# A two-layer diffusion backbone: the seven-product stage with its residual in SBUF and one pair of column blocks per piece

## The chip, the cores and the metric

The kernel runs on one core of a Trainium2 chip. Its engines, as the profile names them, are PE (TensorE; PEld is its loading of weights), DVE (VectorE), ACT (ScalarE), POOL (GpSimd) and SP (SyncE, which here only issues transfers). The metric is the device time of one execution in microseconds (us); of several runs the median counts. A profiled execution is one further run, with its own time; its span goes from the first to the last instruction.

## The reference

Two layers work on 512 latent tokens and 256 context tokens of width 1024. Each layer is a mixing part and a SwiGLU feed-forward part, each behind an RMSNorm whose scale, shift and gate ("modulation") come from `SiLU(cond) @ w_mod`. All is float32. In the last layer the context leaves no output, so only the latent tokens go through its out-projection and feed-forward part. Cut to what matters here:

```python
D_MODEL = 1024; SEQ = 512; CTX_LEN = 256; DEPTH = 2; D_FF = 2816; N_MOD = 6

def swiglu(h, w_gate, w_up, w_down):
    return (jax.nn.silu(h @ w_gate) * (h @ w_up)) @ w_down

def hybrid_layer(x, xc, mod, mod_c, ..., ctx_out):
    sh1, sc1, g1, sh2, sc2, g2 = [mod[:, i] for i in range(N_MOD)]
    ...                                        # three kinds of mixing heads
    x = x + g1 * (jnp.concatenate([y_a, y_b, y_c], axis=-1) @ w_out)
    x = x + g2 * swiglu(modulate(x, norm2_g, sh2, sc2), w_gate, w_up, w_down)
    if ctx_out:                                # the same for xc, in layer 0
        ...
    return x, xc
# for each layer: mod = silu(c) @ w_mod[l] + b_mod[l]; then hybrid_layer; at the end rms_norm(x, final_g)
```

## The kernel before, in words

**Precision.** Every matrix product is made of three: each float32 operand is split into a high part `hi` and a rest `lo`, and TensorE adds hi·hi, hi·lo and lo·hi. For weights, `wload` (L127) does it: SP loads a tile of 128 x 1024 into a slot of the pool `wraw` (four slots), ACT copies it to `whi` (L133), DVE subtracts to get `wlo` (L134); `whi` and `wlo` have three buffers each. `split` (L112 to L114) does the same for tokens and for combined weights.

**Order.** The program is one list of instructions, laid out by hand in Python; each engine runs its part of the list in order, and a tile framework puts in the waits: an instruction that needs a slot of a pool waits until the former user of the slot is done. Transfers queue on the engine that issues them, so a waiting one holds up all behind it.

**Tokens.** The residual x lives in eight tiles, one for each block k of 128 of the 1024 features, with 768 token columns: 256 of the context and 512 latent ones in a tile (`xsl`, L1104, gives a group's columns). `resid` (L1110 to L1114) adds a finished product from PSUM, times the gate row of modulation, onto x, one DVE instruction for each block and token group.

**The seven-product stage** is the feed-forward part of layer 0, `ffn_seven` (L1352). The 2816 columns of w_gate and w_up are 22 blocks of 128, taken in 11 pairs. For a pair, the product of [even, odd feature blocks] by [two column blocks] with the tokens, cut into two halves of 384, is a 2 x 2 block product; it is made with seven block products in place of eight (a Strassen-Winograd scheme). A `Unit` (L1222) does that for the gate (`up` 0) or the up-projection (`up` 1) of one pair: it loads two w_seven tiles, forms sums of weight blocks on DVE (`sums`, L1247; L1250 to L1252), splits them, runs seven products of 12 matmuls 128 x 384 (`prod`, L1265), and puts SiLU(gate) x up into the tiles gh and gl (`put`, L1293). The token operands of the seven products (T1 to T4, B11, B21, B22 for four j) are made once, by `token_sums` and `operands` (L1188, L1196).

After some pairs their part of w_down follows: a *down* (L1360). For each of the eight output blocks k it runs `dense` (L142) over the columns of the piece, two PSUM tiles (512 latent, 256 context columns), alternating between the PSUM pools mm (three tiles) and mx (four), and adds onto x. `FF0_PIECES` (L27) says which pairs go together: one pair, then five times two. The stages of the next unit are woven into the list: its first three products are ahead of the down, the others behind it.

In the stage SBUF is full: the token operands and the gh and gl of two pairs leave no room for x. So x goes to DRAM (`xd`) at the end of the norm (L1178), and in each of the first five downs, for each k, POOL loads `xs` from xd (L1452), DVE adds onto it, and POOL stores it back (L1454). The sixth, last down brings x back (L1461) and runs through `lagged` (L1117): all eight k of the latent tokens, with those of the context trailing behind, so that the next layer's norm of the latent tokens can start while TensorE still works. `TRAIL` says how many trail and after how many of them the norm is begun. Its sums of squares are added on POOL (L264).

**Fill.** The modulation of layer 1 is worked off as filler: `mod_steps` (L210) makes one item for each load of a 128 x 1024 tile of w_mod into a `wraw` slot (L220), one DVE product with accumulated sum (L223), and, for the last of a vector, two small ones. In this stage its items are loaded on POOL's queue. Vectors 0 to 4 of layer 1 (56 items) are issued in the downs: one for each k of the first down, one or two by turns for each k of the next four, 12 in all for each. Vector 5 (8 items) is worked off in layer 1's out-projection, on SP's queue, where `dense` takes one item at each call.

The lines that the diff touches, with the functions that call them:

## Time and profile before

| what | value |
|---|---|
| median of 3 runs | 1766.45 us (1765.04 to 1768.68) |
| profiled execution | 1771.83 us, span 1769.2 us |
| mean granted TensorE clock | 0.965 |
| PE busy | 1641.7 us (93% of the span) |
| DVE busy | 1121.1 us (63%) |
| ACT, POOL busy | 696.3 us (39%), 249.1 us (14%) |
| HBM read, written | 204.31 MB, 26.21 MB |
| the seven-product stage from its first down to the end of its last | 517.58 to 1064.87 us |

How to read the rows that follow: a group names line, engine, operation, `out<-in` by the program's names, shape and count; behind the bar stand its busy time, the mean ns of one, the time that its engine sat idle just ahead of it and what ended that. "Idle" of an engine that is not the bottleneck costs nothing. A row of waits gives the total, how often, and the longest. The granted clock is in shares of full speed, in the page's slices in tenths. Numbers behind a name tell buffers apart.

### The profile page before, as it was taken

Reading aid. Unit: us, or ns where it says so; the run is one execution under the profiler, and the core shown is the slowest. Engines: PE = TensorE matmul, PEld = TensorE weight load, DVE = VectorE, ACT = ScalarE, POOL = GpSimd, SP = SyncE. Lnnn points to the kernel's source line nnn. Section 1 sums busy time; section 2 is a strip of 40 time slices with the busy share of each in tenths; the row PEclk is TensorE's granted clock in tenths of the full one; section 3 lists DMA queues with packets and bytes.
Section 4 is the critical chain, followed back from the end, with each engine's and each line's share of the span. In section 5 each row is a group of like instructions: output and inputs, shape, how many; then the busy total and the mean of one; then the engine's idle time right before and its main releaser. Section 6 shows DMA issues by size and latency. Waiting matters only on the chain.

```text
span 1769.2 us, 26551 instructions
## 1 busy us (share of the span) xinstructions
PE 1641.7 (93%) x10520; PEld 1437.6 (81%) x10520; DVE 1121.1 (63%) x1987; ACT 696.3 (39%) x1277; POOL 249.1 (14%) x309
## 2 busy tenths in 40 slices
PE   7998989899887989899898999989989999999998
PEld 5876777778776969789797988867878988888888
DVE  5598788776875757666575757575597633333335
ACT  5454344643632414133241445534455522222225
POOL 0011022242211020211202030012143100000000
PEclk9998999999897999999898999989999999999999
DMA  8751323234336283653727452211225333222222
GB/s 310 244 152 60 120 79 93 69 117 139 129 120 226 93 272 112 218 186 127 259 79 256 139 185 88 93 57 37 73 91 172 107 99 99 97 99 95 96 78 84
DMA packets 67563, 232.24 MB, mean 131 GB/s; under 512 B 8688, under 2 KB 10352, under 8 KB 67312
## 3 DMA queue, kind: packets, MB, share of 16 engines
q1 hardware_dynamic: 51696, 163.44, 28.2%
q0 software_dynamic: 15744, 67.12, 11.5%
q8 instruction: 82, 1.34, 0.3%
q14 instruction: 41, 0.34, 0.1%
HBM read 204.31 MB, written 26.21 MB: 130 GB/s over the span
## 4 chain that ended last, share of the span: by engine, by line
PE 56%; DVE 15%; issue 14%; DMA 9%; ACT 3%; POOL 2%; DVEq 0%; SPq 0%; POOLq 0%; ACTq 0%
PE dps L157 35%; DMA wmod<-in_w_mod 5%; PE wps L413 4%; PE X L1271 3%; DMA wraw<-in_w_dn 3%; PE vps L659 3%; DVE wlo L134 2%; PE Z L1271 1%; DVE wmod L223 1%; PE ptps L595 1%; PE bops L553 1%; PE Y L1271 1%; DMA wraw<-in_w_seven 1%; PE bsps L553 1%; DVE wlo L114 1%
## 5 line engine op out<-in xcount | busy, mean ns | idle before, releaser
L133 ACT ACTIVATE whi<-wraw 128x1024 fp32r<-128x1024 f32 (+3 forms) x182 | 183.4, 1008 | 511.1 <-PE dps L157 241.0
L134 DVE TENSOR_TENSOR wlo<-wraw,whi 128x1024 fp32r<-128x1024 f32 (+3 forms) x182 | 214.6, 1179 | 155.2 <-ACT whi L133 152.6
L157 PE MATMUL dps<-gh,whi 128*128 128x512 f32 (+1 forms) x576 | 182.0, 359 | 41.0 <-ACT whi L133 41.0
L157 PE MATMUL dps<-gl,whi 128*128 128x512 f32 (+1 forms) x576 | 180.0, 355 | 0.0
L157 PE MATMUL dps<-gh,wlo 128*128 128x512 f32 (+1 forms) x576 | 178.2, 352 | 0.3 <-DVE wlo L134 0.3
L223 DVE SCALAR_TENSOR_TENSOR wmod<-wmod,c_all 128x1024 f32<-128x1024 f32 x96 | 122.6, 1280 | 47.5 <-DMA wmod<-in_w_mod 46.8
L157 PEld LDWEIGHTS dps<-gh,whi 128*128 128x128 f32 x576 | 104.2, 200 | 58.3 <-ACT whi L133 44.2
L157 PE MATMUL dps<-ll,whi 128*128 128x512 f32 x336 | 136.6, 407 | 1.4 <-DVE ll L114 1.4
L157 PE MATMUL dps<-lh,whi 128*128 128x512 f32 x336 | 137.0, 409 | 0.3 <-DVE ck L796 0.3
L157 PE MATMUL dps<-lh,wlo 128*128 128x512 f32 x336 | 135.8, 405 | 0.0
L157 PE MATMUL dps<-h2lh,whi 128*128 128x512 f32 (+1 forms) x336 | 128.0, 384 | 0.0
L157 PE MATMUL dps<-h2ll,whi 128*128 128x512 f32 (+1 forms) x336 | 128.0, 384 | 0.0
L157 PE MATMUL dps<-h2lh,wlo 128*128 128x512 f32 (+1 forms) x336 | 127.9, 384 | 0.0
L157 PEld LDWEIGHTS dps<-gl,whi 128*128 128x128 f32 x576 | 103.8, 199 | 14.8 <-DVE gl L114 0.2
L157 PEld LDWEIGHTS dps<-gh,wlo 128*128 128x128 f32 x576 | 102.8, 197 | 15.3 <-DVE wlo L134 1.2
L1113 DVE SCALAR_TENSOR_TENSOR x<-dps,modT,x 128x256 f32<-128x256 f32 (+1 forms) x80 | 46.9, 589 | 102.5 <-PE dps L157 98.9
L113 ACT ACTIVATE whi<-wraw 128x1024 fp32r<-128x1024 f32 (+1 forms) x66 | 60.0, 914 | 79.9 <-DMA wraw<-in_w_seven 33.3
L157 PE MATMUL dps<-ch,whi 128*128 128x256 f32 x256 | 76.8, 300 | 12.2 <-DVE bv L532 8.0
L1271 PE MATMUL X<-ol,whi 128*128 128x384 f32 x242 | 81.9, 338 | 3.1 <-DVE ol L114 3.1
L1271 PE MATMUL X<-oh,whi 128*128 128x384 f32 x242 | 81.8, 338 | 1.3 <-ACT gate L1290 0.9
L1271 PE MATMUL X<-oh,wlo 128*128 128x384 f32 x242 | 81.5, 337 | 1.0 <-DVE wlo L114 1.0
L157 PE MATMUL dps<-ch,wlo 128*128 128x256 f32 x256 | 75.6, 295 | 3.5 <-DVE wlo L134 3.5
(387 smaller groups left out, 3954.3 us busy)
## 6 DMA issues: line engine op xcount, KB each, us to landing
wmod<-in_w_mod POOLq DMA_DIRECT2D x56, 512.0 KB, 4.6
wraw<-in_w_seven SPq DMA_DIRECT2D x44, 512.0 KB, 4.0
wmod<-in_w_mod SPq DMA_DIRECT2D x40, 512.0 KB, 3.7
wraw<-in_win_blk SPq DMA_DIRECT2D x34, 512.0 KB, 3.6
xs<-xd POOLq DMA_DIRECT2D x40, 384.0 KB, 5.1
xd<-xs POOLq DMA_DIRECT2D x40, 384.0 KB, 5.2
wraw<-in_w_out SPq DMA_DIRECT2D x23, 512.0 KB, 3.3
wraw<-in_w_dn SPq DMA_DIRECT2D x22, 512.0 KB, 4.8
```

The costliest lines, as they stand in the source:

```text
L113: ac.activation(out=hi, in_=src, func=AF.Copy)
L114: ve.tensor_tensor(out=lo, in0=src, in1=hi.bitcast(F32), op=ALU.subtract)
L133: ac.activation(out=hi[:, 0:n], in_=raw[:, 0:n], func=AF.Copy)
L134: ve.tensor_tensor(out=lo[:, 0:n], in0=raw[:, 0:n], in1=hi[:, 0:n].bitcast(F32), op=ALU.subtract)
L157: m = te.matmul(out=ps[:, 0:T], lhsT=wt[:, c], rhs=(flo if wh else fhi)(k), start=(k == 0 and wi == 0), stop=(k == nk - 1 and wi == 2),)
L223: ve.scalar_tensor_tensor(out=wraw.tile([128, D], F32, tag="w", name="junk") if t < ts[-1] else raw, in0=raw, scalar=1.0, in1=c_all[:, t, ...
L413: m = te.matmul(out=ps[:, 0:T], lhsT=wt[:, cs_], rhs=(flo if wh else fhi)(k), start=(k == 0 and wi == 0), stop=(k == KD - 1 and wi == 2))
L553: m = te.matmul(*args, **kw)
L595: te.transpose(out=tps[:, i * 128:(i + 1) * 128], in_=pt[:, i * 128:(i + 1) * 128], identity=ident)
L659: te.matmul(out=vps[i][:, 0:408], lhsT=tokslice(nm, k, i), rhs=wt[:, cs], start=(k == 0 and wi == 0), stop=(k == KD - 1 and wi == 2))
L1113: ve.scalar_tensor_tensor(out=xs, in0=ps, scalar=modT[:, row * 8 + k, g[3]:g[3] + 1], in1=xs, op0=ALU.mult, op1=ALU.add)
L1271: m = te.matmul(out=ps[:, 0:HN], lhsT=wt[:, c], rhs=O[op, j][wh], start=(start and j == 0 and wi == 0), stop=(j == 3 and wi == 2), skip_gr ...
```

## The change

- **Pieces.** `FF0_PIECES` becomes eleven pieces of one pair, so there are eleven downs, ten of the first kind and the last through `lagged`. gh and gl of only one pair are held at a time.
- **Residual.** x stays in its SBUF tiles. The 40 loads and 40 stores of xs, the eight stores of x into xd and the eight loads back go; `resid` adds onto x itself. With eleven downs there are 176 residual adds in the stage where there were 96.
- **w_down's layout.** A 128 x 1024 tile now holds four k of one pair, so a down loads two tiles, each once.
- **Token operands.** For j = 3, T3's hi and lo share one tile, T4 goes into a spare slot (4) of the context's operand tiles, and T1 takes ordinary tiles: 13 tiles of the pool `zc`, none of `za`.
- **Fill.** In the stage only vectors 0 to 2 of layer 1 remain, 40 items, still on POOL's queue: one in each unit and two in each down (at k = 1 and 5). Vectors 3 and 4 (16 items) take the place of vector 5 in layer 1's out-projection, and vector 5 (8 items) goes into the first piece of layer 1's feed-forward part, both on SP's queue.
- **Tail.** `TRAIL[1]`, which the last down uses, goes from (5, 2) to (7, 1).

```diff
-FF0_PIECES = [(0, 2)] + [(f, 4) for f in range(2, 22, 4)]
+FF0_PIECES = [(f, 2) for f in range(0, 22, 2)]
...
-TRAIL = [(7, 1), (5, 2), (4, 2), (4, 2)]
+TRAIL = [(7, 1), (7, 1), (4, 2), (4, 2)]
...
-        def resid(pss, k, row, gs, xt=None):
+        def resid(pss, k, row, gs):
             for ps, g in zip(pss, gs):
-                xs = xsl(k, g) if xt is None else xt[:, goff(g):goff(g) + g[2]]
+                xs = xsl(k, g)
                 ve.scalar_tensor_tensor(
                     out=xs, in0=ps, scalar=modT[:, row * 8 + k, g[3]:g[3] + 1], in1=xs, op0=ALU.mult, op1=ALU.add)
...
-                else:
-                    gp.dma_start(out=xd[k], in_=x[k][:, 0:768])
...
+                if j == 3 and which == "T3":
+                    o3 = zct("o3", F32R)
+                    split(o3[:, n1], o3[:, n2], t[:, n1])
+                    O["T3", j] = (o3[:, n1], o3[:, n2])
+                    split(ch_[:, 4, :], cl_[:, 4, :], t[:, n2])
+                    O["T4", j] = (ch_[:, 4, :], cl_[:, 4, :])
+                    continue
...
                 def dload(k):
-                    if k // 2 not in cache:
-                        cache.clear()
-                        cache[k // 2] = wload(A["w_dn0_%d" % pi][k // 2])
-                    c = (k % 2) * nf * 128
-                    return [t[:, c:c + nf * 128] for t in cache[k // 2]]
+                    if k // 4 not in cache:
+                        cache[k // 4] = wload(A["w_dn0_%d" % pi][k // 4])
+                    c = (k % 4) * nf * 128
+                    return [t[:, c:c + nf * 128] for t in cache[k // 4]]
...
                         u.stage2b()
+                        feed(1)
                         nxt = units[nu + i + 1] if nu + i + 1 < len(units) else None
...
                     for k in range(KD):
-                        xt = zat("xs")
-                        gp.dma_start(out=xt, in_=xd[k])
-                        resid(dense(dload(k), nf, [gpart(g) for g in whole], mm if k % 2 == 0 else mx), k, 5, whole, xt)
-                        gp.dma_start(out=xd[k], in_=xt)
-                        feed(1 + k % 2 if pi else 1)
+                        resid(dense(dload(k), nf, [gpart(g) for g in whole], mm if k % 2 == 0 else mx), k, 5, whole)
+                        if k % 4 == 1:
+                            feed(1)
                     pin[0] = last_pe[0]
                 else:
                     feed(len(fill))
-                    x = x_tiles()
-                    for k in range(KD):
-                        gp.dma_start(out=x[k][:, 0:768], in_=xd[k])
...
-        fill.extend(mod_steps(l, (5,)))
+        fill.extend(mod_steps(l, (3, 4) if last else (5,)))
...
-            fill.extend(mod_steps(1, range(5), True))
+            fill.extend(mod_steps(1, range(3), True))
...
         hp2 = [hpart(h2, g) for g in groups]
-        while fill:
-            fill.pop(0)()
+        feed(len(fill))
+        fill.extend(mod_steps(1, (5,)))
```

How this moves instructions, at the places that matter. First DVE, where the second down begins. Before, ahead of that down's first residual add and behind it (L1300 and L1296 are the last unit's `put`, L134 the w_down split, L223 a modulation item, L1113 a residual add):

```order
L134 TENSOR_TENSOR wlo<-wraw,whi 128x1024
L114 TENSOR_TENSOR gl<-gate,gh 128x384
L1296 TENSOR_TENSOR sn<-sn,Z 128x384
L223 SCALAR_TENSOR_TENSOR wmod,modT<-wmod,c_all 128x1024
L1300 TENSOR_TENSOR gate<-gate,sn 128x384
L114 TENSOR_TENSOR gl<-gate,gh 128x384
L223 SCALAR_TENSOR_TENSOR wmod,modT<-wmod,c_all 128x1024 x2
L1113 SCALAR_TENSOR_TENSOR xs<-dps,modT,xs 128x512
L1113 SCALAR_TENSOR_TENSOR xs<-dps,modT,xs 128x256
L134 TENSOR_TENSOR wlo<-wraw,whi 128x1024
```

And in the change (the lines of `put` are now L1305 and L1301):

```order
L134 TENSOR_TENSOR wlo<-wraw,whi 128x1024
L114 TENSOR_TENSOR gl<-gate,gh 128x384
L1301 TENSOR_TENSOR sn<-sn,Z 128x384
L223 SCALAR_TENSOR_TENSOR wmod,modT<-wmod,c_all 128x1024
L1305 TENSOR_TENSOR gate<-gate,sn 128x384
L114 TENSOR_TENSOR gl<-gate,gh 128x384
L134 TENSOR_TENSOR wlo<-wraw,whi 128x1024
L223 SCALAR_TENSOR_TENSOR wmod,modT<-wmod,c_all 128x1024
L1113 SCALAR_TENSOR_TENSOR x_4159<-dps,modT,x_4159 128x512
L1113 SCALAR_TENSOR_TENSOR x_4159<-dps,modT,x_4159 128x256
L114 TENSOR_TENSOR wlo<-wraw,whi 128x1024
```

The place of the `put` is the same; the second w_down split comes ahead of the first residual add, and one item has left the place ahead of it. Further on in the same down of the change, between the add of block 3 and that of block 7, stand the next unit's split and its sums of weight halves (L1255 to L1257):

```order
L114 TENSOR_TENSOR wlo<-wraw,whi 128x1024
L1113 SCALAR_TENSOR_TENSOR x_4163<-dps,modT,x_4163 128x512
L1113 SCALAR_TENSOR_TENSOR x_4163<-dps,modT,x_4163 128x256
L1255 TENSOR_TENSOR s_5880<-wraw 128x512
L1113 SCALAR_TENSOR_TENSOR x_4164<-dps,modT,x_4164 128x512
L1113 SCALAR_TENSOR_TENSOR x_4164<-dps,modT,x_4164 128x256
L1256 TENSOR_TENSOR s_5881<-s_5880,wraw 128x512
L1257 TENSOR_TENSOR wraw<-wraw 128x512
L1113 SCALAR_TENSOR_TENSOR x_4165<-dps,modT,x_4165 128x512
L1113 SCALAR_TENSOR_TENSOR x_4165<-dps,modT,x_4165 128x256
L223 SCALAR_TENSOR_TENSOR wmod,modT<-wmod,c_all 128x1024
```

They are the next unit's work, which DVE now has within the shorter down. Second POOL's queue. Before, in the first downs, loads and stores of xs stand among the items:

```order
L1452 DMA xs<-xd 128x768 x2
L220 DMA wmod<-in_w_mod 128x1024 x4
L1454 DMA xd<-xs 128x768
L220 DMA wmod<-in_w_mod 128x1024 x2
L1454 DMA xd<-xs 128x768
```

In the change POOL's queue in the stage, from the sums of squares of the norm ahead of it to those of the last down, reads:

```order
L264 TENSOR_TENSOR sqacc<-sqacc,sq 128x256 x6
L220 DMA wmod<-in_w_mod 128x1024 x40
L645 MEMSET v_9617 128x12
L645 MEMSET v_9618 128x12
L645 MEMSET v_9619 128x12
L264 TENSOR_TENSOR sqacc<-sqacc,sq 128x512 x6
```

All transfers of x have gone from it, and nothing else has come in their place.

More of the change, by code (lines that the diff above doesn't have):

```diff
@@ L1203, in operands @@
                 else:
-                    hi, lo = [(zat if j == 3 else zct)(nm, F32R)[:, 0:2 * HN] for nm in ("oh", "ol")]
+                    hi, lo = [zct(nm, F32R)[:, 0:2 * HN] for nm in ("oh", "ol")]
                 split(hi, lo, t[:, 0:2 * HN])
@@ L1352, in ffn_seven @@
         def ffn_seven():
-            nonlocal x
             pairs = [p for f0, nf in FF0_PIECES for p in range(f0 // 2, (f0 + nf) // 2)]
@@ L1617, in layout @@
         "w_seven": np.stack([blocks(w)[0].reshape(22, 128, 8, 128)[:, :, KORD].reshape(22, 128, 1024) for w in (wg, wu)]),
-        **{"w_dn0_%d" % i: blocks(wd[:, f * 128:(f + n) * 128])[0].reshape(4, 2, 128, n * 128).transpose(0, 2, 1, 3).reshape(
-            4, 128, 2 * n * 128) for i, (f, n) in enumerate(FF0_PIECES)},
+        **{"w_dn0_%d" % i: blocks(wd[:, f * 128:(f + n) * 128])[0].reshape(2, 4, 128, n * 128).transpose(0, 2, 1, 3).reshape(
+            2, 128, 4 * n * 128) for i, (f, n) in enumerate(FF0_PIECES)},
         "win_av": ksplit(wi[:, :, 256:512], 4), "w_out": blocks(I["w_out"]), "w_gate": blocks(wg), "w_up": blocks(wu),
```

## The prediction

> **What bounds the kernel now.** I read the page first, for the engine shares, the clock and the transfers.
>
> ```profile
> PE 1641.7 (93%) x10520; PEld 1437.6 (81%) x10520; DVE 1121.1 (63%) x1987; ACT 696.3 (39%) x1277; POOL 249.1 (14%) x309
> PEclk9998999999897999999898999989999999999999
> wmod<-in_w_mod POOLq DMA_DIRECT2D x56, 512.0 KB, 4.6
> xs<-xd POOLq DMA_DIRECT2D x40, 384.0 KB, 5.1
> ```
>
> TensorE is busy for 93%, so what it loses is the rest, and the slices where its clock falls below 9 count too, because there it is busy but slow. Of the six such slices three, the deepest among them, lie between 517 and 977 us, in the seven-product stage. Next comes the view that splits time windows by engine, cut at the starts and ends of the downs (the dense second half of each piece) and of the units between them. Its columns are the length, busy time and count of PE, PEld, DVE, ACT and POOL, the granted clock, the DMA share and GB/s.
>
> ```profile
> 517.58:550.52 32.94, 21.73 (x97) 18.31 (x97) 18.04 (x30) 3.33 (x5) 10.07 (x19) 0.79 0.74 245
> 550.52:615.70 65.18, 62.02 (x340) 61.33 (x339) 45.35 (x73) 28.36 (x48) 3.53 (x7) 0.95 0.37 122
> 615.70:660.26 44.56, 36.38 (x193) 30.93 (x191) 25.69 (x41) 5.55 (x6) 12.00 (x22) 0.92 0.80 270
> 660.26:719.86 59.60, 58.89 (x338) 58.45 (x337) 43.75 (x68) 26.73 (x46) 3.27 (x6) 1.00 0.35 116
> 719.86:765.76 45.90, 38.16 (x194) 32.58 (x194) 25.69 (x41) 5.67 (x6) 12.00 (x22) 0.89 0.80 263
> 765.76:826.20 60.44, 58.92 (x339) 58.44 (x338) 44.10 (x72) 26.96 (x46) 3.27 (x6) 1.00 0.35 114
> 826.20:872.24 46.04, 38.47 (x193) 32.88 (x193) 24.77 (x40) 5.67 (x6) 12.01 (x22) 0.89 0.81 262
> 872.24:931.72 59.48, 58.79 (x338) 58.47 (x337) 44.66 (x70) 26.96 (x46) 3.27 (x6) 1.00 0.36 116
> 931.72:977.00 45.28, 38.67 (x194) 32.93 (x194) 25.97 (x42) 4.65 (x6) 12.00 (x22) 0.89 0.81 267
> 977.00:1029.97 52.97, 51.46 (x297) 50.99 (x296) 36.33 (x59) 25.13 (x41) 4.57 (x11) 1.00 0.46 153
> 1029.97:1064.87 34.90, 34.90 (x203) 30.34 (x202) 20.52 (x30) 16.14 (x27) 14.03 (x11) 1.00 0.49 162
> ```
>
> The units run with TensorE nearly full. The five downs that pass x through DRAM (rows 1, 3, 5, 7 and 9, together 214.7 us, nine pairs) have the clock at 0.79 to 0.92 and the DMA engines at 0.74 to 0.81. The sixth, which keeps x in SBUF, has neither fault. The groups of instructions on TensorE and the waits of every engine in the stage say what is late; the last row is from the waits of SP's DMA queue alone.
>
> ```profile
> L157 PE MATMUL dps<-gh,whi 128*128 128x512 f32 (+1 forms) x342 | 102.0, 369 | 41.0 <-ACT whi L133 41.0
> ACT whi L133 <- DMA wraw<-in_w_dn: 148.5, 15, 14.8
> POOL xs L1452 <- DMA xd<-xs: 73.6, 24, 7.3
> SPq L130 <- DVE wmod L223: 207.9, 15, 19.0
> ```
>
> TensorE waits 41.0 us for split weights, the split waits for the w_dn load, and that load is not issued until a modulation item gives its wraw slot back. The items themselves queue on POOL behind the x transfers. The chain of waits, inside the second down, shows one round of it (start, length, what): item, its product, and only then the load of weights, eleven us from end to end.
>
> ```profile
> 622.80 4.44 DMA wmod<-in_w_mod
> 627.33 1.24 DVE wmod L223 x2
> 628.63 5.45 DMA wraw<-in_w_dn
> ```
>
> **The change, part by part.** *The downs.* I take the unhindered speed from TensorE's timeline; a row "x2" is one 512-column and one 256-column matmul.
>
> ```profile
> 518.64 0.51 PE L157 MATMUL dps<-gh,whi 128*128 128x512 f32 x2
> 519.68 0.51 PE L157 MATMUL dps<-gh,whi 128*128 128x512 f32 x2
> ...
> 545.66 0.84 PE L157 MATMUL dps<-gh,wlo 128*128 128x512 f32 x2
> 548.22 0.73 PE L157 MATMUL dps<-gh,whi 128*128 128x512 f32 x2
> ```
>
> Three pairs of matmuls take 519.68 − 518.64 = 1.04, so 0.347 each. A down of one column pair has 8 k × 2 blocks × 3 products = 48 of them: 16.6 us. After a stall they run at (548.22 − 545.66) / 4 = 0.64. Of the nine pairs' 214.7 us, 9 × 16.6 = 149.8 is work and 64.9 is loss: 41.0 of idle time and 23.9 mostly at the slow rate.
>
> What held the loads goes away by three edits with one answer: the 80 transfers of xs and 16 of x leave POOL's queue, only 4 modulation items are issued per pair (one per unit, two per down) where a two-pair down issued 12 within itself, and a down needs two w_dn loads, queued right behind the w_seven loads. The bytes of w_dn stay about the same. I take the whole loss away: **−64.9**.
>
> *The units.* The three windows of four full units at clock 1.00 give 59.48 to 60.44; the one behind the first down took 65.18, with starved splits at its start. All at the best value: 297.7 (rows 2, 4, 6, 8, 10) to 4 × 59.48 + 52.97 = 290.9, **−6.8**. Per unit the DVE has about what it had (some 44 us per four units) plus one item of 1.31 each (1.223 and the read of its accumulator, 0.08), so 49 of 59.5: covered by TensorE, and 1.3 per unit if that cover failed.
>
> *New friction at ten downs.* What DVE does in a down comes from its groups by shape in the stage:
>
> ```profile
> L1113 DVE SCALAR_TENSOR_TENSOR xs<-dps,modT,xs 128x512 f32<-128x512 f32 x40 | 29.9, 749 | 21.3 <-PE dps L157 16.6 <-DMA xs<-xd 4.4
> L1113 DVE SCALAR_TENSOR_TENSOR xs<-dps,modT,xs 128x256 f32<-128x256 f32 x40 | 19.0, 475 | 0.0
> L134 DVE TENSOR_TENSOR wlo<-wraw,whi 128x1024 fp32r<-128x1024 f32 x22 | 27.2, 1235 | 28.9 <-ACT whi L133 28.9
> L223 DVE SCALAR_TENSOR_TENSOR wmod<-wmod,c_all 128x1024 f32<-128x1024 f32 x56 | 68.3, 1223 | 46.5 <-DMA wmod<-in_w_mod 46.2
> L1252 DVE TENSOR_TENSOR wraw<-wraw 128x512 f32<-128x512 f32 x21 | 14.4, 683 | 0.0
> ```
>
> From its first to its last add a down of one pair now has 8 × (0.749 + 0.475) = 9.8 of adds (per pair twice as many, since each add took in two pairs), two splits for the next unit 2.5, two items 2.6 and three sums of weight halves 2.0: 16.9, for 16.6 of TensorE. Neighbours overlap by some 0.07 (below: 1.23 long, and the next starts 1.16 later), 1.6 over 23 instructions, which leaves about 1.3 of slack. Ahead of the first add stand the last `put`, one split and one item, and PSUM lets TensorE run two k (4.2 us) ahead of the adds. Lower bound of what is lost: 0. Upper bound: one split and one item, 2.5, plus the first add's 0.75, so about 3 per down, if the item's load comes late. The second down of before starts behind much the same order:
>
> ```profile
> 612.68 1.23 DVE L223 SCALAR_TENSOR_TENSOR wmod<-wmod,c_all 128x1024 f32<-128x1024 f32 x1 [0.30 <-DMA wmod<-in_w_mod]
> 613.84 0.56 DVE L1300 TENSOR_TENSOR gate<-gate,sn 128x384 f32<-128x384 f32 x1
> ```
>
> The item held DVE there just ahead of the `put` that the down needs, and its load made DVE wait only 0.30, so I stay nearer the lower bound: 1.0 at each of ten downs, **+10** (0 to 30).
>
> *The tail.* The last down has one pair now and its sums of squares stay on POOL:
>
> ```profile
> L264 POOL TENSOR_TENSOR sqacc<-sqacc,sq 128x512 f32<-128x512 f32 x6 | 8.6, 1440 | 15.6 <-ACT sq L263 15.6
> ```
>
> A k of the 512 latent columns takes 6 × 0.347 × 512 / 768 = 1.39 for one pair, just less than POOL's 1.44: eight adds now end behind TensorE, where two pairs (2.8) left POOL idle between adds. TRAIL (7, 1) leaves seven context denses of 0.7 behind, one of them ahead of the wait. If nothing hides it: 0.4 of accumulated lag, ACT's square, one add and the scale, some 4 twice. I take **+4** (0 to 8).
>
> *Layer 1.* Sixteen modulation items more run there, on SP's queue, 8 more in the out-projection and 8 in the first FFN piece: 16 × 1.31 = 21 us of DVE.
>
> ```profile
> 1360.00:1380.00 20.00, 20.00 (x171) 20.00 (x169) 9.91 (x13) 8.07 (x13) 9.67 (x8) 1.00 0.42 134
> 1480.00:1769.00 289.00, 282.99 (x1398) 238.89 (x1396) 108.62 (x134) 85.07 (x121) 0.00 (x0) 1.00 0.28 92
> ```
>
> DVE has 10 of 20 free there, and over half of the FFN, with TensorE full: nearly all is covered. What is queued behind a waiting item is the next w_out load on SP's queue, and behind its product on DVE the split of that load, so the upper bound is half the 21: **+2** (0 to 10). The 13 packed operand tiles cost one split more, ahead of the first down; I put it at nothing.
>
> *Sum*: −64.9 − 6.8 + 10 + 4 + 2 = −55.7. The profiled execution took 1771.83, 5.4 above the runs' median of 1766.45; 1771.8 − 55.7 = 1716.1, less 5.4 is **1710 us**.
>
> **The rivals.** *A: w_dn is still late.* All three kinds of load still share four slots, so the second w_dn tile can wait for an item. For it: the 207.9 us that SP's queue waited were for items. Against: an item now meets no x transfers. One stall per down, of the shortest of the old ten:
>
> ```profile
> 739.56 0.81 PE L157 MATMUL dps<-gh,whi 128*128 128x512 f32 x2 [2.79 <-ACT whi L133]
> 740.16 0.84 PE L157 MATMUL dps<-gl,whi 128*128 128x512 f32 x2
> ```
>
> Each costs 2.8 and its slow matmuls, 23.9 / 10 = 2.4: 10 × 5.2 − 10 = 42 more, 1752 us. The Trainium skill, "TensorE: Matmul & The Clock Gate", Part 1, puts the fall to half clock behind about 3.4 us of idleness; by that such stalls would cost their idle time alone, which would make A an estimated 1728. The trace disagrees: behind 2.79 us the matmuls run at 0.6 to 0.66.
>
> *B: DVE sets the downs.* If the 16.9 of the means is the truth, nothing is left to catch up in, and the 2.5 of split and item come back as a PSUM wait at each down: 10 × 2.5 − 10 = 15 more, 1725 us. Against: the overlap of neighbours, which the rows show.
>
> *C: the wait moves to layer 1.* 16 items share the slots with w_out and FFN weights there. In the downs, 64.9 us were lost around 56 items, 1.16 each: 16 × 1.16 − 2 = 17 more, 1727 us. Against: the eight that ran there before left TensorE full.
>
> *D, the slower side: short PSUM waits halve the clock in the downs.* With DVE this tight TensorE can pause at every second k, and matmuls at 0.64 instead of 0.347 cost 0.293 each. Slower than before begins where the gain, 55.7 / 10 = 5.6 per down, is eaten: 19 of 48 slow. With half of each down slow, 240 × 0.293 = 70 more, it would take 1780 us. Against: stalls like this one, in the units, left their windows at 0.95 to 1.00.
>
> ```profile
> 556.57 0.69 PE L1271 MATMUL X<-olh,wlo 128*128 128x384 f32 x1 [0.98 <-DVE wlo L114]
> ```
>
> The Trainium skill, same page, "A second HAM failure mode: psum-queue depth-cycling", tells of this in another kernel: pauses between groups, each short, made the clock oscillate. No run here shows it yet.
>
> The downs of before have no stall of this kind, so their rows can't exclude D; it gets little.
>
> **How the numbers follow.** Forecast 0.60, A 0.12 (1752), B 0.14 (1725), C 0.08 (1727), D 0.06 (1780). This kernel's times tell about 0.2% (3.5 us) from no change. A to C and the forecast are faster; one in a hundred goes from A, and one from D, to no change, the rest of D to slower: faster 0.93, same 0.02, slower 0.05. Low end: friction, tail and layer 1 at nothing give 1694, and up to 4 more if the units' start stalls vanish, so 1690. High end: beyond C and the friction's upper bound (1730), and into A, 1745. That leaves out most of A and D.
>
> **What would show it.** Right: no idle time of the downs' matmuls behind L133, ten downs of 16.6 to 18 us with clock 1.00, their DMA share near the units' 0.35, POOL's queue with modulation items alone. A shows as TensorE idle for L133 again; B as DVE at full in the downs and TensorE idle for a residual add; C as TensorE idle for weights between the out-projection and the first FFN piece; D as clock under 0.95 in downs whose stalls are all short. The tail shows as idle time before the sum-of-squares matmul at the end of layer 0. The forecast is wrong if the downs sum to over 200 us, or if the units grow.

## The result

| what | before | after |
|---|---|---|
| median | 1765.74 us (4 runs) | 1708.88 us (4 runs, 1707.05 to 1712.0) |
| ratio, 95% interval | | 0.9677, 0.9658 to 0.9695 |
| profiled execution, span | 1771.83, 1769.2 us | 1707.05, 1705.4 us |
| mean granted TensorE clock | 0.965 | 0.983 |

The change makes the kernel 3.2% faster; the forecast was 1710 us. From the page of the changed kernel, the slices of the clock and the transfers that have changed:

```profile
PEclk9998999999899999999999999989999999999999
wmod<-in_w_mod POOLq DMA_DIRECT2D x40, 512.0 KB, 3.8
wraw<-in_w_dn SPq DMA_DIRECT2D x22, 512.0 KB, 3.3
```

The dips of the clock in the stage are gone, an item of the stage lands in 3.8 us instead of 4.6, a w_dn tile in 3.3 instead of 4.8. TensorE's group of the downs' first product, up to the last down, and the windows by stage (the columns are those of the prediction; first two of the ten downs, then the last unit with the wait behind it and the last down, then two of the nine windows of two units):

```profile
L157 PE MATMUL dps<-gh,whi 128*128 128x512 f32 x160 | 63.7, 398 | 0.7 <-DVE x L1113 0.5
```

```profile
512.88:529.56 16.68, 16.68 (x97) 14.69 (x97) 15.20 (x25) 3.13 (x5) 1.06 (x2) 1.00 0.50 159
652.19:669.75 17.56, 17.52 (x97) 14.78 (x97) 16.38 (x26) 3.38 (x5) 1.06 (x2) 1.00 0.47 150
...
948.59:973.71 25.12, 21.39 (x123) 20.75 (x121) 15.36 (x27) 11.04 (x19) 0.37 (x3) 1.00 0.32 106
973.71:999.67 25.96, 24.84 (x121) 20.92 (x121) 14.13 (x23) 11.82 (x22) 12.08 (x11) 0.87 0.28 101
529.56:558.90 29.34, 29.34 (x170) 29.34 (x169) 21.06 (x34) 12.80 (x22) 1.06 (x2) 1.00 0.29 91
576.02:605.37 29.35, 29.35 (x171) 29.35 (x169) 20.23 (x34) 12.74 (x22) 1.05 (x2) 1.00 0.27 90
```

TensorE no longer waits for split w_dn weights at all (41.0 us before). The ten downs sum to 171.55 us, 17.2 each, at clock 1.00; the units are full. What is left lies behind them: in the row of the last down (973.71 to 999.67) the clock is 0.87.

To set the terms of the sum against the traces a mark is needed that both have behind the stage. It is TensorE's first wait for L686 in layer 1, here from its timelines, before and after:

```profile
1149.15 0.82 PE L693 MATMUL rowps<-cst,f 128*64 128x128 f32 x6 [1.85 <-DVE f L686]
```

```profile
1083.87 0.81 PE L693 MATMUL rowps<-cst,f 128*64 128x128 f32 x6 [1.85 <-DVE f L686]
```

| term | forecast | measured | how |
|---|---|---|---|
| downs, at nine pairs | −64.9 + 10 | −59.8 | 214.7 to 171.55 − 16.64 |
| units | −6.8 | −11.4 | 297.7 to 286.3, without the stall at 973.71 |
| tail | +4 | +10.6 | end of the last unit to the mark: 119.18 to 113.17, and one pair (16.64) less in it |
| layer 1 | +2 | +1.5 | mark to the end: 620.05 to 621.53 |
| ahead of the first down | 0 | −4.7 | 517.58 to 512.88 |

They add up to the 63.8 us between the two spans. The last row is no gain of the change: 4.5 of the 4.7 us were there in the same matmul at 388.8 and 384.3, ahead of every transfer that the change takes away (the first starts at 405.0), and in the variants below the first down began anywhere between 511.8 and 518.2. The forecast's 5.4 us between the profiled execution of before and the median stood for this.

### The profile page after: what moved, and what is told of

The parts are those of the page before. It is cut to its first block, busy times and chain, and to the rows that moved or that the text cites. A ratio compares the mean times of both kernels' runs of the same rounds, so it can differ in the third digit from the quotient of the medians.

```text
span 1705.4 us, 26357 instructions
## 1 busy us (share of the span) xinstructions
PE 1617.9 (95%) x10520; PEld 1418.7 (83%) x10520; DVE 1156.9 (68%) x2064; ACT 693.9 (41%) x1274; POOL 184.8 (11%) x197
## 4 chain that ended last, share of the span: by engine, by line
PE 68%; DVE 15%; issue 8%; DMA 3%; ACT 3%; POOL 2%; DVEq 0%; SPq 0%; POOLq 0%; ACTq 0%
PE dps L157 40%; PE X L1276 8%; PE wps L413 3%; PE Z L1276 3%; PE vps L659 3%; DMA wmod<-in_w_mod 3%; PE Y L1276 2%; DVE wlo L134 2%; PE ptps L595 1%; DVE wmod L223 1%; PE bops L553 1%; PE bsps L553 1%; DVE junk L223 1%; DVE nm L580 1%; ACT whi L133 1%
## 5 line engine op out<-in xcount | busy, mean ns | idle before, releaser
L133 ACT ACTIVATE whi<-wraw 128x1024 fp32r<-128x1024 f32 (+2 forms) x178 | 180.9, 1017 | 357.5 <-PE dps L157 237.0
L134 DVE TENSOR_TENSOR wlo<-wraw,whi 128x1024 fp32r<-128x1024 f32 (+2 forms) x178 | 212.5, 1194 | 122.6 <-ACT whi L133 117.9
L1113 DVE SCALAR_TENSOR_TENSOR x<-dps,modT,x 128x512 f32<-128x512 f32 (+1 forms) x240 | 136.8, 602 | 88.7 <-PE dps L157 87.7
L157 PE MATMUL dps<-gh,whi 128*128 128x512 f32 (+1 forms) x576 | 173.2, 346 | 4.3 <-ACT gh L113 3.0
L157 PE MATMUL dps<-gh,wlo 128*128 128x512 f32 (+1 forms) x576 | 170.6, 341 | 0.0
L157 PE MATMUL dps<-gl,whi 128*128 128x512 f32 (+1 forms) x576 | 170.4, 341 | 0.0
L223 DVE SCALAR_TENSOR_TENSOR wmod<-wmod,c_all 128x1024 f32<-128x1024 f32 x96 | 122.5, 1277 | 20.2 <-DMA wmod<-in_w_mod 19.8
L157 PE MATMUL dps<-lh,wlo 128*128 128x512 f32 x336 | 135.0, 402 | 0.0
L157 PEld LDWEIGHTS dps<-gl,whi 128*128 128x128 f32 x576 | 97.7, 189 | 13.3 <-DVE gl L114 0.5
L157 PEld LDWEIGHTS dps<-ll,whi 128*128 128x128 f32 x336 | 65.0, 193 | 16.2 <-issue 2.2
L114 DVE TENSOR_TENSOR wlo<-wraw,whi 128x1024 fp32r<-128x1024 f32 (+1 forms) x66 | 69.8, 1058 | 11.5 <-ACT whi L113 11.5
L157 PEld LDWEIGHTS dps<-lh,whi 128*128 128x128 f32 x336 | 64.7, 193 | 14.9 <-issue 1.9
```

The costliest lines, as they stand in the source:

```text
L114: ve.tensor_tensor(out=lo, in0=src, in1=hi.bitcast(F32), op=ALU.subtract)
L133: ac.activation(out=hi[:, 0:n], in_=raw[:, 0:n], func=AF.Copy)
L134: ve.tensor_tensor(out=lo[:, 0:n], in0=raw[:, 0:n], in1=hi[:, 0:n].bitcast(F32), op=ALU.subtract)
L157: m = te.matmul(out=ps[:, 0:T], lhsT=wt[:, c], rhs=(flo if wh else fhi)(k), start=(k == 0 and wi == 0), stop=(k == nk - 1 and wi == 2),)
L223: ve.scalar_tensor_tensor(out=wraw.tile([128, D], F32, tag="w", name="junk") if t < ts[-1] else raw, in0=raw, scalar=1.0, in1=c_all[:, t, ...
L1113: ve.scalar_tensor_tensor(out=xs, in0=ps, scalar=modT[:, row * 8 + k, g[3]:g[3] + 1], in1=xs, op0=ALU.mult, op1=ALU.add)
```

## The experiments

**Which edit did it: the fill or the transfers of x?** The prediction gave one answer for three edits. Four kernels take them apart. First the fill alone, on the kernel before:

```diff
                         u.stage2b()
+                        feed(1)
...
-                        feed(1 + k % 2 if pi else 1)
+                        if k % 2 == 1 and (pi or k % 4 == 1):
+                            feed(1)
...
-            fill.extend(mod_steps(1, range(5), True))
+            fill.extend(mod_steps(1, range(3), True))
```

(and vectors 3 to 5 in layer 1 as in the change).

> The kernel before with the change's fill alone: 40 items in the stage, one per unit, two in the first down and four in each two-pair down, and the other 16 and 8 moved into layer 1 as in the change; x still goes through DRAM, pieces of two pairs stay. Theory P (items hold the wraw slots and queue behind the x transfers; it takes both to make w_dn late): TensorE's idle time for split w_dn weights falls from 41.0 to 5 to 15 us, the downs from 214.7 to about 175, the time to 1720 to 1735. Rival S (the number of items in four slots is all of it): idle under 5, time 1712 to 1720. Rival R (the x transfers keep the DMA engines busy and so make the loads slow, whatever the items do): idle stays above 25, time 1745 or more.

Measured: 1712.6 us, ratio 0.9709 (0.9690 to 0.9729). TensorE's group in its stage, and one of its two-pair downs:

```profile
L157 PE MATMUL dps<-gh,whi 128*128 128x512 f32 (+1 forms) x352 | 99.1, 344 | 9.1 <-DVE xs L1113 9.0
```

```profile
602.68:637.42 34.74, 33.97 (x193) 29.35 (x193) 22.43 (x34) 5.24 (x7) 8.66 (x16) 1.00 0.80 257
```

No wait for weights is left, with all 80 transfers in place and the DMA engines as busy as before (0.80); the 9.0 us left are for residual adds. The thinner fill alone brings 52 of the 57 us. That is what S had forecast, in idle time and in time; P had expected 5 to 15 us of idle time and 1720 or more. R falls: busy DMA engines by themselves were not what made the weights late.

Next the opposite, the dense fill of before in the changed kernel:

```diff
-                        if k % 4 == 1:
+                        if k % 4 != 3:
                             feed(1)
...
-            fill.extend(mod_steps(1, range(3), True))
+            fill.extend(mod_steps(1, range(5), True))
```

(without the item per unit, and with layer 1's fill as before).

> The changed kernel with the fill of before: 56 items in the downs, six in each one-pair down, none in the units, and only 8 items in layer 1 (out-projection). x stays in SBUF. Theory P: an item without x transfers ahead of it turns its slot round in about 4.5 + 1.3 us, so w_dn is late by less than before: idle for split weights 10 to 25 us, time 1725 to 1740. Rival S: idle near 41 and the slow clock back, 1750 or more. Rival R: no idle for weights, time 1706 to 1714; DVE's 6 items of 1.3 us in a 16.6 us down then show as PSUM waits only.

Measured: 1711.44 us, ratio 0.9697 (0.9679 to 0.9715):

```profile
L157 PE MATMUL dps<-gh,whi 128*128 128x512 f32 (+1 forms) x352 | 96.3, 347 | 6.0 <-ACT gh L113 3.0 <-DVE x L1113 2.6
```

No wait for weights here either, so S falls too as it was put, and P had the size wrong: dense items beside the change's other edits cost some 2.5 us, not 16 to 31. R had this time in its range, but the run before has ruled out its mechanism. Then the stores of x put back into the changed kernel, and then both together:

```diff
                         resid(dense(dload(k), nf, [gpart(g) for g in whole], mm if k % 2 == 0 else mx), k, 5, whole)
+                        gp.dma_start(out=xd[k], in_=x[k][:, 0:768])
```

> The changed kernel with 80 stores of x (384 KB each) into DRAM put back on POOL's queue, one after each residual add of the ten downs; nothing reads them. The count of x transfers in the downs is that of before (40 loads and 40 stores). Theory P: with only two items per down behind them little is late: idle for split weights under 8 us, time 1709 to 1722. Rival R: DMA share in the downs back at 0.7 or more and w_dn loads over 5 us, idle above 20 us, 1735 or more.

> The changed kernel with both undone in part: the dense fill of before (six items in each one-pair down) and the 80 stores of x on POOL's queue. What stays of the change is the piece of one pair with two w_dn loads, and that nothing reads x back. Theory P (it takes dense items and x transfers on one queue): TensorE's idle time for split w_dn weights comes back, 20 us or more, and the time is 1735 or more. Rival L (the layout: two loads per down that land ahead of it, where four came within it): idle under 5 us and the time within 4 us of the dense fill alone (1711).

Measured: 1712.18 us, ratio 0.9702 (0.9684 to 0.9720), for the stores alone; 1735.84 us, ratio 0.9843 (0.9793 to 0.9892), for both. A down of the first, and a down, a window of two units and TensorE's groups in the units of the second:

```profile
610.80:627.95 17.15, 17.12 (x98) 14.70 (x98) 15.94 (x26) 3.33 (x5) 4.71 (x9) 1.00 0.81 289
```

```profile
665.40:683.12 17.72, 17.47 (x97) 14.69 (x97) 15.28 (x26) 2.50 (x3) 5.16 (x10) 1.00 0.80 283
780.81:812.59 31.78, 29.89 (x171) 29.23 (x170) 24.29 (x38) 13.88 (x23) 2.41 (x5) 1.00 0.43 155
```

```profile
L1276 PE MATMUL X<-olh,wlo 128*128 128x384 f32 x95 | 33.5, 353 | 6.5 <-DVE wlo L114 6.5
L1276 PE MATMUL X<-olh,whi 128*128 128x384 f32 x95 | 33.5, 353 | 8.0 <-ACT whi L113 7.9
```

| pieces of one pair | 40 items | 56 items in the downs |
|---|---|---|
| no x transfers on POOL | 1708.9 | 1711.4 |
| 80 stores of x on POOL | 1712.2 | 1735.8 |

Alone, either costs some 3 us, which the intervals do not tell from nothing (the changed kernel's own repetition, below, took 1711.5); together they cost 27. So it does take both to make weights late here, as P said. But what comes late then are the w_seven weights of the units (31.8 us for two units instead of 29.3; of the 27 us, 20 lie in the units and 7 in the downs), not w_dn: the group of the downs has no idle time for L133 in any of the four. That is rival L in its idle time, not in its time, which it had put within 4 us of 1711. With pieces of one pair a down needs only two tiles, the second of them at 8.3 us, when four k are done. In the changed kernel both are split by 2.4 us into the down. With the dense fill the second is loaded within the down and gets there with little to spare. The rows are of the second down of before, which began at 615.37, and of the down at 665.40 of the kernel with both undone:

```profile
621.27 1.23 DVE L134 TENSOR_TENSOR wlo<-wraw,whi 128x1024 fp32r<-128x1024 f32 x1 [0.49 <-ACT whi L133]
```

```profile
671.26 1.22 DVE L134 TENSOR_TENSOR wlo<-wraw,whi 128x1024 fp32r<-128x1024 f32 x1
```

Both are done 7.1 us into the down. What a down of the change does not have is a third and a fourth tile. The stalls of before were theirs; in its second down they came at these times:

```profile
635.21 0.62 PE L157 MATMUL dps<-gh,whi 128*128 128x512 f32 x2 [2.87 <-ACT whi L133]
...
649.46 1.00 PE L157 MATMUL dps<-gh,whi 128*128 128x512 f32 x2 [5.01 <-ACT whi L133]
```

Without its stall the first is 17.0 us into the down, where four k of two pairs (4 × 4.16 = 16.6) are done and the third of four tiles is due; the second is the fourth tile. Each of the four two-pair downs stalled just twice, and so did the first (at 529.71 and 544.21), which has one pair, but in four tiles of half the width. So it was the third and fourth tiles that were late, and the changed downs have none. No run put back the loads of x, or had pieces of two pairs without transfers of x.

**Is it POOL's queue, or the four slots?** In the kernel before, the items' loads were put on SP's queue, away from the x transfers:

```diff
-            (gp if single else sp).dma_start(out=raw, in_=A["w_mod"][l, v, i])
+            sp.dma_start(out=raw, in_=A["w_mod"][l, v, i])
```

> The kernel before with one edit: the items of the stage are loaded on SP's queue, where they stand among the w_dn loads (three items ahead of each), instead of on POOL's behind the x transfers. Theory P: items no longer wait for x transfers, a slot turns round in 4 to 6 us, and idle for split weights falls from 41.0 to under 15, time 1725 to 1740. Rival S (items in four slots hold w_dn up, whichever queue they come by): idle stays at 30 or more, time 1755 to 1775, since w_dn now also queues behind the items.

Measured: 1756.7 us, ratio 0.9951 (0.9929 to 0.9973).

```profile
L157 PE MATMUL dps<-gh,whi 128*128 128x512 f32 (+1 forms) x352 | 101.3, 356 | 28.0 <-ACT whi L133 27.3 <-DVE xs L1113 0.7
```

Idle time of 27.3 us is neither under 15 nor over 30; the time is in S's range. A third of the wait went with POOL's queue in these profiles, of one execution each; by the medians on this chip (1764.15 before) 7 us of the 57 did. The larger part stays, with items and w_dn in the same slots. (On SP the items also stand directly ahead of w_dn, so this is no clean measure of the slots alone.)

**What a stall costs.** Extra in-place maxima (g = max(g, g), which change no value) were put into the last put ahead of nine downs, 3 in the first to 11 in the last:

```diff
                 ve.tensor_tensor(out=g, in0=g, in1=ps[:, 0:HN] if d is None else d, op=ALU.mult)
+                if q == 1:
+                    for _ in range(self.delay):
+                        ve.tensor_tensor(out=g, in0=g, in1=g, op=ALU.max)
```

> The changed kernel with 3 to 11 extra in-place DVE instructions (g = max(g, g), 128 x 384, about 0.55 us each) in the last put ahead of the second to tenth down, so that TensorE meets a stall of growing length at the start of each. From the rows of before (2.18 and 2.79 us were followed by slow matmuls, 0.7 to 1.5 us were not): stalls up to 1.5 us leave the clock alone, those of 2.2 us and more are followed by 3 to 5 us at the half clock, and cost up to 2.4 us beyond their length. By the Trainium skill's 3.4 us only the last two or three would.

Measured (one run): 1779.86 us, and stalls of 2.12, 2.59, 3.95, 5.42, 6.44, 8.61, 9.19, 9.88 and 10.34 us. TensorE's rows behind the first, the second and the last:

```profile
562.51 1.19 PE L157 MATMUL dps<-gh,whi 128*128 128x512 f32 x5 [2.12 <-ACT gh L113]
563.54 0.53 PE L157 MATMUL dps<-gl,whi 128*128 128x512 f32 x2
563.90 0.51 PE L157 MATMUL dps<-gh,wlo 128*128 128x512 f32 x2
...
611.51 1.20 PE L157 MATMUL dps<-gh,whi 128*128 128x512 f32 x5 [2.59 <-ACT gh L113]
...
614.25 0.84 PE L157 MATMUL dps<-gh,whi 128*128 128x512 f32 x2
614.89 0.84 PE L157 MATMUL dps<-gl,whi 128*128 128x512 f32 x2
...
1005.53 1.01 PE L157 MATMUL dps<-gh,whi 128*128 128x512 f32 x2 [10.34 <-ACT gh L113]
...
1008.25 0.84 PE L157 MATMUL dps<-gl,whi 128*128 128x512 f32 x2
1009.42 0.51 PE L157 MATMUL dps<-gh,whi 128*128 128x512 f32 x2
```

Behind 2.12 us the pairs follow at 0.35; behind 2.59 and all longer ones at 0.64, for some 4 to 5.5 us, whether the stall was 2.59 or 10.34. The downs behind those eight took 18.4 to 19.3 us where the changed kernel's took 17.2. So a long stall costs its length and some 2 us more, and those 2 don't grow with it. No stall of this run was shorter than 2.12, so it does not test the expected bound of 1.5.

**The tail.** The prediction put it down to POOL's sums of squares (Q). The trace after shows something else at the start of the last down (TensorE, then DVE):

```profile
973.71 1.39 PE L157 MATMUL dps<-gh,whi 128*128 128x512 f32 x3 [3.01 <-ACT gh L113]
974.89 0.63 PE L157 MATMUL dps<-gl,whi 128*128 128x512 f32 x1
```

```profile
971.22 0.55 DVE L1301 TENSOR_TENSOR sn<-sn,Z 128x384 f32<-128x384 f32 x1
971.68 0.95 DVE L134 TENSOR_TENSOR wlo<-wraw,whi 128x768 fp32r<-128x768 f32 x1
972.55 0.55 DVE L1305 TENSOR_TENSOR gate<-gate,sn 128x384 f32<-128x384 f32 x1
973.69 0.56 DVE L114 TENSOR_TENSOR gl<-gate,gh 128x384 fp32r<-128x384 f32 x1 [0.59 <-ACT gh L113]
```

At every other down the next unit's products lie between the last `put` and the down. Here there is no next unit, and in the kernel before there were two pairs in the last down, the first of them long ready. On top of it DVE splits the next layer's first weights (128 x 768) in the middle of that `put`: the framework puts a queue together by what is ready, and may place an instruction ahead of its place in the Python list, as this order shows. Four kernels on one chip, first the changed one as a base, then one edit each; the last reverses gh, gl and the columns of w_dn in the last down and puts the 768-wide split behind the `put`:

> The changed kernel once more, on the same chip as the three tail variants that follow, as their base: 1709 us, ratio to the kernel before near 0.968.

```diff
-TRAIL = [(7, 1), (7, 1), (4, 2), (4, 2)]
+TRAIL = [(7, 1), (5, 2), (4, 2), (4, 2)]
```

> The changed kernel with TRAIL[1] back at (5, 2). Theory Q (my term for the tail: POOL's sums of squares end behind TensorE): two context denses more lie behind the wait on POOL only if the norm is begun later, so the 0.58 us of idle ahead of the sum-of-squares matmul goes, but the next layer's wave starts later: within 2 us of the changed kernel. Rival U (the tail's loss is the last put, which no unit covers: TensorE waits 3.01 us for gh and runs slow after it): no difference in that stall, time the same within 2 us. It tells only whether TRAIL matters.

```diff
-                    lagged(dload, nf, gpart, 5, done, *TRAIL[1], eng=gp)
+                    lagged(dload, nf, gpart, 5, done, *TRAIL[1], eng=ve)
```

> The changed kernel with the sums of squares of the last down added on DVE in place of POOL. Theory Q: the idle time ahead of the sum-of-squares matmul and that ahead of the next wave go, 2 to 4 us less. Rival U: at most 1 us less, since the 3.01 us stall and its slow matmuls stay.

```diff
+                if pi == len(FF0_PIECES) - 1:
+                    gh.reverse()
+                    gl.reverse()
...
+        if held_put[0] is not None and n == 768:
+            after(iv, held_put[0])
```

> The changed kernel with two edits at the start of the last down: it takes the column block that the last put does not write first, and the split of the next layer's first weights (128 x 768) is ordered behind that put on DVE (it stood ahead of it, 0.95 us). Rival U: the 3.01 us stall falls to about 1.3, under the length from which the clock falls, so the slow matmuls behind it (2 us) go too: 3 to 4 us less than the changed kernel. Theory Q: the stall was not what ends the tail; under 1 us less.

| kernel | median us | ratio (95%) | last unit's start to the mark, profile |
|---|---|---|---|
| change, again | 1711.5 | 0.9684 (0.9655 to 0.9713) | 135.0 |
| TRAIL (5, 2) | 1711.9 | 0.9677 (0.9649 to 0.9706) | 131.2 |
| squares on DVE | 1710.4 | 0.9679 (0.9652 to 0.9707) | 135.4 |
| last put | 1707.8 | 0.9654 (0.9625 to 0.9683) | 131.3 |

Q falls: with the sums on DVE nothing is gained. (That run alone is not clean, since there TensorE waited 1.7 us for residual adds on DVE, 0.6 in the changed kernel; but in the changed kernel no wait for POOL stands ahead of the sum-of-squares matmul, at 989.72.) The two edits at the last put take the whole 3.01 us stall away, more than the 1.7 expected, and make the stretch 4 us shorter; the times lean the same way, by 3 to 4 us, with intervals that overlap. TensorE's idle time in the stretch fell by 1.1 us only, since other waits grew; the rest goes with the clock, which stood at half twice for 3.41 us in the base and not at all here. TRAIL (5, 2) looked 4 us shorter in its one profile and is not in its times; its profile too has no such fall. In the eight kernels that keep the stall, the stretch goes with the number of these falls of 3.41 us: 131.2 us with none, 133.7 with one, 135.0 to 135.4 with two, 135.8 and 136.2 with three. To see whether it adds anything to the other:

> The changed kernel with the two edits at the last put and TRAIL[1] at (5, 2). If the two losses of the tail are separate (the uncovered put, 3 us and what the clock adds; the norm begun while POOL still adds, up to 1 us of waits and what the clock adds), the profile's stretch from the start of the last unit to the first rows of layer 1 is 5 to 8 us shorter than the changed kernel's 135, and the time 1701 to 1705, ratio near 0.964. If (5, 2) was worth nothing by itself and only met no clock fall in its one profile, the time is that of the last-put variant, ratio near 0.9655.

Measured: 1705.83 us, ratio 0.9653 (0.9628 to 0.9679); its stretch was 130.6 us. That is the last-put variant's ratio, so TRAIL (5, 2) is worth nothing that can be seen. These two variants are the fastest kernels run, ahead of the changed one by some 0.3%, which the intervals do not settle.

**The friction of the downs.** On top of the last kernel, the two items of each down went into the units:

```diff
                         u.stage2b()
-                        feed(1)
+                        feed(2)
...
-                        if k % 4 == 1:
-                            feed(1)
```

> The same, with the 20 items of the downs moved into the units (two in each, none in a down). If my friction term of the downs is DVE's order there (items among the residual adds), the ten downs fall from 17.15 to 16.7 us each, 4 to 5 us less. If it is PSUM and overlap at the start and end of a down, nothing changes, or the units grow by what the downs lose.

Measured: 1712.66 us, ratio 0.9696 (0.9672 to 0.9720): 7 us more, where 4 to 5 less or nothing was expected. The units stayed at 29.34 us for two; the downs grew (the longest of the ten, and the units behind it):

```profile
703.68:722.04 18.36, 17.66 (x97) 14.67 (x97) 16.37 (x28) 2.60 (x4) 1.59 (x3) 1.00 0.44 133
722.04:751.38 29.34, 29.34 (x170) 29.34 (x169) 20.47 (x32) 13.73 (x23) 1.06 (x2) 1.00 0.28 97
```

All ten together took 177.7 us, where the kernel without this edit had 172.9. The waits of DVE in the stage, first this kernel, then the changed one:

```profile
DVE s L1259 <- DMA wraw<-in_w_seven: 14.6, 10, 2.1
DVE wmod L227 <- DMA wmod<-in_w_mod: 8.1, 10, 1.1
```

```profile
DVE wmod L223 <- DMA wmod<-in_w_mod: 7.0, 14, 0.9
```

Items in the units take slots from the next unit's w_seven tiles. Their loads now land 1.5 us late in each of ten downs, and the sums of weight halves that wait for them stand on DVE among the residual adds. What TensorE pays shows in the waits of its weight loads (PEld), whose next matmul needs a PSUM tile that a residual add has not yet left: in the stage, the changed kernel, the kernel ahead of this edit, and this one:

```profile
PEld dps L157 <- DVE x L1113: 4.8, 17, 0.6
PEld dps L161 <- DVE x L1117: 6.4, 18, 0.8
PEld dps L161 <- DVE x L1117: 10.5, 33, 1.2
```

Above ten times 16.64 their downs took 5.2, 6.5 and 11.3 us. So the friction is this wait: DVE has some 1.3 us of slack in a down (15.9 busy of 17.2), and whatever makes its adds late takes from it. Of the 7 us, 5 are here; in the two profiles the stretch behind the mark is 2.1 longer too, whose cause stays open.

## Why the prediction was right

*What bounds the kernel.* Right: split w_dn weights, late because modulation items held the slots, and a clock that fell behind nearly every stall (not behind that of 2.87 us at 635.21). All 41.0 us of idle time are gone and the clock is 1.00 in the downs.

*The downs' term, −64.9.* Right in size, and the reason was right as far as it went: dense items and x transfers make the weights late only together. But the step "three edits with one answer" hid that fewer would have been enough here: the fill alone gives 1712.6, and pieces of one pair with x in SBUF give 1711.4 with the old fill. The third of them, the layout with two tiles per down, was given half a clause ("queued right behind the w_seven loads") and keeps w_dn on time even with the dense fill and 80 stores of x; the units then pay. The part put on POOL's queue was too large: taking the items off it gave back 7 of the 57 us.

*Friction, +10.* Too much: ten downs took 17.2 instead of 16.6, 5 us in all, inside the bounds of 0 to 30. The mechanism was right: the 5 us are the 4.8 that weight loads waited for residual adds, and the variant that made DVE wait 1.5 us more in each down lost 4.9 there, which is rival B's mechanism, from another wait.

*Units, −6.8.* Too little. They were reckoned at the best window of before, 59.5 for four; with no stalls of 0.7 to 1.5 us at their start two units take 29.35, so 58.7 for four. The trace of before had those stalls; they were allowed for in the low end only.

*Tail, +4.* The step that failed: it named POOL's sums of squares and a wait ahead of the sum-of-squares matmul. No such wait is there (the 0.58 us that the expectation of the TRAIL run calls so stands ahead of a dense matmul, at 988.64, and is for a residual add), and DVE in POOL's place changed nothing. The tail lost 10.6. TensorE's idle time from the end of the last unit to the mark went from 2.5 to 8.6 us: 3.0 more is the last `put` without a unit behind it, 3.1 are short waits between the last down and the next layer's first matmuls (0.3 to 1.5 us each in the trace, one of 2.9 in the repeated run). Twice the clock stood at half for 3.41 us, from 973.8 behind the `put` and from 990.9, which costs up to 1.7 us each; in the kernel before it did not fall there. The last 1 us is not traced. That a last down of two pairs had covered the short waits is argued from the rows; no run took them away.

*Layer 1, +2.* 1.5 in the two profiles. The stretch was 617.8 to 620.2 in the four kernels with the old fill of layer 1 and 618.3 to 623.1 in the ten with the new, so the size is not settled; C (17 us) is excluded.

A and D did not happen: no idle time for L133, no clock under 1.00 in any of the ten downs, where the 17 waits for residual adds lasted 0.6 us at most. The errors of friction and units (+5 and +5) and of the tail (−7) went against each other, and the 5.4 for the profiled execution met a like difference by chance (1716.1 less 5.4 is 1710.7, put down as 1710). So it is luck that the sum came out within 2 us; it was better than its terms.

## What to carry to other kernels

A transfer that waits for a buffer slot can be freed from several sides (fewer users of the slot, a shorter queue ahead of those users, or a layout that needs fewer tiles while the crowd is there), and the gains don't add: try the cheapest edit alone first. Here a few lines of fill order brought 52 of 57 us, without any of the repacking. When the last piece of a pipeline is made shorter, look at what the longer one had covered: the last operand's latency and the chain into the next stage.

## What the runs showed of the hardware

The same stall did not always cost the same. In eight kernels TensorE waited 3.01 to 3.02 us at the last down. In five (the changed kernel, its repetition, the dense fill, dense fill with stores, the stalls of growing length) slow matmuls followed; in three (stores alone, TRAIL, squares on DVE) they went on at full speed:

```profile
979.22 0.84 PE L157 MATMUL dps<-gh,whi 128*128 128x512 f32 x3 [3.01 <-ACT gh L113]
979.90 0.41 PE L157 MATMUL dps<-gl,whi 128*128 128x512 f32 x1
```

The clock's records in the traces show a grid. In each of the 14 profiled executions all stretches at half clock that begin and end in it last 3.41 us or a whole multiple, and they begin whole multiples of 3.41 us apart: with the stalls of growing length, at 613.3, 664.5, 715.7 and 770.3, which is 15, 15 and 16 steps. Here are TensorE's windows on that grid around the stall, first in the changed kernel, then with the stores alone (length, busy time and count of PE, clock, DMA share, GB/s):

```profile
970.37:973.79 3.42, 0.41 (x3) 1.00 0.43 125
973.79:977.20 3.41, 3.41 (x9) 0.50 0.44 147
```

```profile
974.27:977.68 3.41, 1.94 (x12) 1.00 0.10 15
977.68:981.09 3.41, 1.87 (x9) 1.00 0.70 228
981.09:984.51 3.42, 3.42 (x19) 1.00 0.28 108
```

In the first the whole stall fell into one window, and the next ran at half clock; in the second it fell across two, 1.5 us in each, and the clock stayed. So it is in all eight: the five that slowed had 2.1 to 3.0 us of idle time in one window, the three others at most 1.9 in any. This is not the whole rule: at 990.9 in the changed kernel the clock fell after a window with 0.7 us idle, in which TensorE ran narrow matmuls of the norm.

In the kernel before, a stall of 3.37 us was followed by four pairs at full speed and only then, at the next step of its grid (968.5), by slow ones:

```profile
966.95 0.62 PE L157 MATMUL dps<-gh,whi 128*128 128x512 f32 x2 [3.37 <-ACT whi L133]
967.40 0.52 PE L157 MATMUL dps<-gl,whi 128*128 128x512 f32 x2
...
968.47 0.79 PE L157 MATMUL dps<-gh,wlo 128*128 128x512 f32 x2
969.06 0.84 PE L157 MATMUL dps<-gh,whi 128*128 128x512 f32 x2
```

So for a stall between 2.1 and 3.4 us it is chance, by where it falls on the grid, whether the clock falls, and a single profile of a variant can look 2 us better for it at each such place, as that of TRAIL (5, 2) did. The Trainium skill, "TensorE: Matmul & The Clock Gate", Part 1, says that the window is free-running; this agrees with it. Its figure of about 3.4 us of idleness is not a bound from which on the clock falls: 2.59 us was enough here.
